# HGRN2 chunk scores: four decay levels in two visits of two levels each, with 88 and 56 query columns

## The chip, the cores and the metric

The kernel runs on one core of a Trainium2 chip. A core has five engines with queues of their own: TensorE (PE, matrix products, with its weight loads shown as PEld), VectorE (DVE), ScalarE (ACT), GpSimd (POOL) and SyncE (SP, which here issues the loads from memory). Their instructions run in the order of each queue and wait for each other through semaphores. Operands lie in the on-chip memory SBUF; TensorE writes its results to PSUM, here in tiles of 128 x 512 that each take a bank, and VectorE and ScalarE read them from there.

The metric is the device time of one launch in microseconds (us); smaller is better.

## The reference: a two-layer trunk, of which the second layer's mixer matters here

The program computes a trunk of two layers on 512 tokens of width 1024: a Mamba-2 mixer, then an HGRN2 mixer, each followed by a normalisation, a squared-ReLU MLP, another normalisation and a gated embedding. Only the HGRN2 mixer is touched. It has 8 heads, 128 wide in keys and in values, and works in chunks of the sequence:

```python
q, fz, v, g = jnp.split(u @ w_in, 4, axis=-1)
log_f = jnp.logaddexp(jnp.log(lb), jnp.log1p(-lb) + jax.nn.log_sigmoid(fz))
k = (1.0 - lb) * jax.nn.sigmoid(-fz)
...
diff = b_[:, :, None] - b_[:, None, :]          # b_: running sum of log_f
dec = jnp.exp(jnp.where(mask, diff, -jnp.inf))
scores = jnp.einsum('blhk,bshk,blshk->bhls', q_, kk, dec)
o = jnp.einsum('bhls,bshv->blhv', scores, v_) + jnp.einsum('blhk,bhkv->blhv', q_ * jnp.exp(b_), s_prev)
```

The score of query token l and key token s (s not after l) is the sum over 128 features of q, k and the product of the forget gates f of the tokens after s up to l. The gates differ by feature, so the decay cannot be taken out of the sum; the outputs are the causal products of scores and values, with a state passed on between chunks.

## The kernel before

Nearly all of the time goes to projections: products of 128 x 128 weights with 512 tokens, each taken as three products of rounded parts (`mm3`, lines 118 to 121, PSUM tiles `pj`). A weight block is loaded (`raw`), rounded by ScalarE (`whi`, line 113), and the remainder is formed by VectorE (`wlo`, line 115).

The HGRN stage runs with an order on TensorE that is written out by hand. `background` (line 903) is one long chain of projections, cut into steps of three matmuls: queries, gates and keys of head h (`qf`), values and output gates (`vg`), and the first half of the output projection (`out0`). `hcore` does the rest for one pair of heads and gives way at each `yield`; the number that it yields (from `FILL`) is how many microseconds' worth of projection steps stand on TensorE before its next part. There are four pairs; for the last one the numbers are multiplied by `LAST`, 0.78. On the other engines a planner sets the order from the program's order, its priorities and the buffers' lives.

`qf` leaves three tiles for a head, all 128 features by 512 tokens: q in a buffer `xs`, the gates f in `sz`, the keys kk in `cv`.

In `hcore` the decay is built up by levels. At level m the tokens stand in blocks of half = 2^m, and neighbouring blocks form a pair. `qd` holds each query times the gates of its own block up to it, kk each key times the gates after it in its block, and `tot` the product of the gates of every block. A key in the first block of a pair and a query in the second one then need no further factor: their scores are a plain matrix product. After level m VectorE multiplies the keys of each first block by the total of the second (line 985), the queries of each second block by the total of the first (line 986), and the totals pairwise (line 988); that makes the state for level m + 1. There are seven levels (half = 1 to 64) in a chunk of 128 tokens.

The products of levels 0 to 4 are done in groups of 32 tokens, 16 groups per head: the keys of a group are the stationary operand (128 x 32), its queries the moving one. I call the 32 matmuls of both heads at one level a visit:

- first visit (line 951): 48 columns, 32 of them the undecayed queries (for the diagonal) and 16 every second one of `qd` (level 0). The two sets lie side by side in the 48-wide `xs` buffer; line 942 copies the 16 into it.
- levels 1 to 4 (line 965): 16 columns each, the second blocks of every pair.
- levels 5 and 6 (line 972): 32 x 32 and 64 x 64 products.

The results go to one PSUM bank per head (`py0`, `py1`). Which of a group's 32 x 32 entries belong to the level is told by a mask: a predicated copy (lines 996 and 1000) takes them from PSUM into `scb`, 128 x 4 x 32 per head. After level 4 ScalarE copies `scb` into the score matrix `sc` (line 1008), and those of levels 5 and 6 come straight from PSUM (line 1014). Then come transposes of the keys (line 1021), the chunk states (lines 1032 to 1037), outputs (lines 1045 to 1047, which read `sc` and `qd`), the norm (lines 1052 to 1057) and transposes of the result (line 1065).

Each level yields 2.94, so that about 12 to 15 projection matmuls stand between two visits, and in that time VectorE does lines 985, 986, 988, 996 and 1000 of the level.

Of the kernel before, what the change touches and what calls it, by code (L numbers as in the profile page):

```python
# [15 lines left out]
P = 128  # L16
# [28 lines left out]
def trunk(ctx: ExitStack, tc, a):  # L45
# [27 lines left out]

    two = dict(xs=2, sz=2, cv=2, cm=2, cbm=2)
    mlp = dict(r=8, blk=2, sg=2)
    bufs = dict(ssd=dict(two, ss=2), mlp0=mlp, hgrn=dict(two, xs=3, sz=4, cv=4, y=2, pv=2, btok=2, sg=2, sc=2, scb=2, qd=2), mlp1=mlp)
    phase = []

    def begin(name):
# [116 lines left out]
        nc.sync.dma_start(b, a["ln"][2 * i + 1 : 2 * i + 2, :].to_broadcast([P, D]))  # L196
        return g, b

    def layer_norm(c, gb, sums=None):

        src = acc[:, c, :]
        mv = mk(sm, [P, 2], "lnmv")
        sd = mk(sm, [P, 1], "lnsd")
        if sums is None:
            st = mk(sm, [P, 2, 6], "lnst")
            for h in range(2):
                nc.vector.bn_stats(st[:, h, :], src[:, h * 512 : (h + 1) * 512])
            nc.vector.bn_aggr(mv, st.rearrange("p a b -> p (a b)"))
            nc.scalar.activation(sd, mv[:, 1:2], AF.Sqrt, bias=eps)
        else:  # L210

            nc.vector.tensor_scalar(mv[:, 0:1], sums[:, c, 0:1], sums[:, c, 1:2], -1.0 / D, ALU.add, ALU.mult)
            sq = mk(sm, [P, 2], "lnsq")
            for h in range(2):
                nc.scalar.activation(
                    tmp("sg", [P, T]), src[:, h * 512 : (h + 1) * 512], AF.Square, bias=mv[:, 0:1], accum_out=sq[:, h : h + 1]
                )
# [60 lines left out]
    def norm(i):  # L278

        gb = ln_params(i)  # L280
        h_s = Split(8)
        sums = mk(sm, [P, NCH, 2], "lnsum") if i else None

        def chunk(c):
            with tc.high_priority(offset=SOON if c < 2 or i % 2 == 0 else 0):
                layer_norm(c, gb, sums)

        return h_s, chunk, lambda c: transpose_split(acc[:, c, :], h_s, c), sums

# [528 lines left out]
    begin("hgrn")  # L818


    lmask = mk(cpool, [P, 6, 32], "lmask", U8)
# [46 lines left out]
    def qf(h):  # L868
        ps = []
        for w in range(2):  # L870
            hi, lo = unit(a["whq"][2 * h + w])
            ps.append(bank(psj, "pj"))
            for k in range(8):
                c = slice(k * P, (k + 1) * P)
                mm3(ps[w], hi[:, c], lo[:, c], x_s.h(k), x_s.l(k), k == 0, k == 7)
                yield 0.65
            if w == 0:

                q = tmp("xs", [P, T // 32, 48])
                nc.scalar.copy(q[:, :, :32], blocks32(ps[0]))  # L880
        f = tmp("sz", [P, T])
        nc.scalar.activation(f, ps[1], AF.Sigmoid)
        nc.scalar.activation(f, f, AF.Identity, scale=lbc[:, h : h + 1], bias=lb[:, h : h + 1])
# [48 lines left out]
    def hcore(h0, s, i0):  # L932
# [3 lines left out]
        q, f, kk = ([need("qf", h0 + r)[n] for r in R] for n in range(3))  # L936
        py = lambda r: bank(psy, "py%d" % r)
        tokens = lambda c, b: (slice(b, b + 32), slice(c * P + b, c * P + b + 32))
        qd = [tmp("qd", [P, T]) for r in R]
        for r in R:  # L940
            nc.vector.tensor_mul(blocks32(qd[r]), q[r][:, :, :32], blocks32(f[r]))
            nc.vector.tensor_copy(q[r][:, :, 32:], blocks32(qd[r])[:, :, 1::2])


        pcs = [py(r) for r in R]
        for r in R:
            for c in range(NCH):
                for b in range(0, P, 32):
                    bs, ts = tokens(c, b)
                    at = slice(c * 48, c * 48 + 48)  # L950
                    nc.tensor.matmul(pcs[r][bs, at], kk[r][:, ts], q[r][:, ts.start // 32], start=True, stop=True)
        tot = f
        tots = [tmp("y", [P, T]) for r in R]
        toff = 0
        for m in range(NLEV):
            half = 1 << m
            if m == NLEV - 2:
                pcs = [py(r) for r in R]
            for r in R if m else ():
                if m < NLEV - 2:  # L960
                    for c in range(NCH):
                        for b in range(0, P, 32):
                            bs, ts = tokens(c, b)
                            at = slice(128 + 64 * m + 16 * c, 128 + 64 * m + 16 * c + 16)
                            nc.tensor.matmul(pcs[r][bs, at], kk[r][:, ts], second(qd[r][:, ts], half), start=True, stop=True)  # L965
                else:

                    for c2 in range(0, NCH, 2):
                        at = slice(base(half) + half * c2 // 2, base(half) + half * (c2 // 2 + 1))
                        for b, c in ((b, c2 + odd) for b in range(0, P, 2 * half) for odd in range(2)):  # L970
                            s0, l0, row = c * P + b, c * P + b + half, b + half * (c - c2)
                            nc.tensor.matmul(
                                pcs[r][row : row + half, at],
                                kk[r][:, s0 : s0 + half],
                                qd[r][:, l0 : l0 + half],
                                start=True,
                                stop=True,
                            )
            nb = T // (2 * half)
            nt = []  # L980
            for r in R:
                qv = qd[r].rearrange("p (b two u) -> p b two u", two=2, u=half)
                kv = kk[r].rearrange("p (b two u) -> p b two u", two=2, u=half)
                tv = tot[r].rearrange("p (b two) -> p b two", two=2)
                nc.vector.tensor_mul(kv[:, :, 0, :], kv[:, :, 0, :], bc(tv[:, :, 1], 2, half))
                nc.vector.tensor_mul(qv[:, :, 1, :], qv[:, :, 1, :], bc(tv[:, :, 0], 2, half))
                nt.append(tots[r][:, toff : toff + nb])
                nc.vector.tensor_mul(nt[r], tv[:, :, 0], tv[:, :, 1])
            toff += nb
            tot = nt  # L990
            for r in R:
                sc, scb, pc = scs[r], scbs[r], pcs[r]
                if m < NLEV - 2:
                    if m == 0:
                        pc = pc[:, : 48 * NCH].rearrange("p (c l) -> p c l", c=NCH)
                        nc.vector.copy_predicated(scb, bc(lmask[:, NLEV - 2, :], 1, NCH), pc[:, :, :32])
                        pc = pc[:, :, 32:]
                    else:
                        pc = pc[:, 128 + 64 * m : 192 + 64 * m].rearrange("p (c l) -> p c l", c=NCH)
                    nc.vector.copy_predicated(  # L1000
                        scb.rearrange("p c (b two u) -> p c b two u", two=2, u=half)[:, :, :, 1, :],
                        bc(second(lmask[:, m, :], half), 1, NCH),
                        pc.rearrange("p c (b u) -> p c b u", u=half),
                    )
                    if m == NLEV - 3:
                        for b in range(0, P, 32):
                            bs = slice(b, b + 32)
                            nc.scalar.copy(sc[bs, :, bs], scb[bs])
                else:
                    pc = pc[:, base(half) : base(half) + 2 * half].rearrange("p (c l) -> p c l", c=2)  # L1010
                    for b in range(0, P, 2 * half):
                        for odd in range(2):
                            row = b + half * odd
                            nc.scalar.copy(sc[b : b + half, odd::2, b + half : b + 2 * half], pc[row : row + half])
            yield FILL[0]

        kt = []
        for r in R:
# [71 lines left out]
def _levels():  # L1090

    i = np.arange(P)
    out = np.zeros((P, 6, 32), np.float32)
    for m in range(5):
        s, l = (i[:, None] % 32) >> m, i[None, :32] >> m
        out[:, m, :] = (s % 2 == 0) & (l == s + 1)
    out[:, 5, :] = i[:, None] % 32 == i[None, :32]
    return out


# [105 lines left out]
```

## Time and profile before

| quantity | value |
|---|---|
| median of 3 runs | 1428.69 us (1428.59 to 1429.52) |
| profiled execution | 1427.82 us, of which the span of the trace is 1426.0 us |
| granted TensorE clock | 1.00 |
| TensorE busy | 1416.5 us, 99% of the span |
| VectorE / ScalarE busy | 1040.9 us / 746.1 us |
| HGRN pairs, about | 833 to 1015 us of the span |

The trace is one execution. A row of the timeline gives start, duration, engine, line, operation, the tiles written and read, shape, and how many equal ones were merged; in brackets stands how long the engine had been idle before it and what ended that. Durations overlap, since an engine begins an instruction before the last one has ended: the distance between two starts tells what an instruction holds its engine for. A single-precision matmul stands in the trace as two records, so a visit of 32 matmuls has 64. A row of the groups gives line, engine, operation, shapes and number, then busy time in all and the mean of one in ns, then the idle time before. A row of waits gives the total, the number and the longest.

### The profile page before, as it was taken

How to read it: one execution, taken by the hardware profiler on the slowest of the kernel's cores; microseconds unless marked ns; L12 is line 12 of the kernel's file. 1: busy time of each engine (PE TensorE's matmuls, PEld its weight loads, DVE VectorE, ACT ScalarE, POOL GpSimd, SP SyncE). 2: the span in 40 equal slices, each digit the busy share in tenths (PEclk: the TensorE clock that was granted, in tenths of full speed). 3: DMA queues.
4: the chain of work that ended last, by engine and by line, in shares of the span. 5: the costliest groups of instructions: out<-in, count | busy, mean ns of one | idle time of the engine just before them, and what ended most of it. 6: DMA issues, size and time to landing. Idle time of an engine off the chain costs nothing.

```text
span 1426.0 us, 20980 instructions
## 1 busy us (share of the span) xinstructions
PE 1416.5 (99%) x8381; PEld 1174.3 (82%) x8381; DVE 1040.9 (73%) x1664; ACT 746.1 (52%) x1118; POOL 1.9 (0%) x12
## 2 busy tenths in 40 slices
PE   9999999999999999999999999999999999999998
PEld 7888888888888888888888878777898888888887
DVE  8998687797967667687977556657685867667873
ACT  7776454563264444545546546555555454544641
POOL 0000000000000000000000000000000000000000
PEclk9999999999999999999999999999999999999999
DMA  8332323233333443434621422122163434434231
GB/s 315 134 124 91 122 84 126 97 118 132 134 119 133 148 141 140 145 136 176 208 74 48 147 76 75 60 90 90 45 234 107 148 133 148 148 133 162 89 119 45
DMA packets 49394, 178.04 MB, mean 125 GB/s; under 512 B 5520, under 2 KB 6288, under 8 KB 49168
## 3 DMA queue, kind: packets, MB, share of 16 engines
q1 hardware_dynamic: 49296, 176.69, 35.3%
q8 instruction: 66, 1.08, 0.3%
q14 instruction: 32, 0.26, 0.1%
HBM read 174.51 MB, written 2.16 MB: 124 GB/s over the span
## 4 chain that ended last, share of the span: by engine, by line
PE 94%; DVE 3%; ACT 2%; DMA 0%; issue 0%; SPq 0%; ACTq 0%; DVEq 0%
PE pj L119 24%; PE pj L120 23%; PE pj L121 23%; PE py L119 5%; PE py L121 5%; PE py L120 5%; PE py L735 1%; PE py L741 1%; PE pm L705 1%; PE py L965 1%; PE pt L233 1%; DVE wlo L115 1%; PE pt L693 1%; PE py L1045 0%; DMA r<-in_w 0%
## 5 line engine op out<-in xcount | busy, mean ns | idle before, releaser
L113 ACT CAST whi<-raw 128x1024 fp32r<-128x1024 f32 x222 | 232.9, 1051 | 346.0 <-PE pj L120 232.8
L119 PE MATMUL pj<-b,whi 128*128 128x512 f32 (+1 forms) x1006 | 382.8, 381 | 0.7 <-ACT b L237 0.7
L120 PE MATMUL pj<-b,whi 128*128 128x512 f32 (+1 forms) x1006 | 380.5, 378 | 0.6 <-DVE b L238 0.6
L121 PE MATMUL pj<-b,wlo 128*128 128x512 f32 (+1 forms) x1006 | 379.3, 377 | 0.0
L115 DVE TENSOR_TENSOR wlo<-raw,whi 128x1024 fp32r<-128x1024 f32 x222 | 269.9, 1220 | 142.2 <-ACT whi L113 136.8
L120 PEld LDWEIGHTS pj<-b,whi 128*128 128x128 f32 x1006 | 189.5, 188 | 33.6 <-issue 0.9
L121 PEld LDWEIGHTS pj<-b,wlo 128*128 128x128 f32 x1006 | 189.4, 188 | 33.7
L119 PEld LDWEIGHTS pj<-b,whi 128*128 128x128 f32 x1006 | 189.0, 188 | 33.9 <-ACT b L237 0.9
L119 PE MATMUL pj<-whi,b 128*128 128x512 f32 x536 | 213.4, 399 | 0.0
L121 PE MATMUL pj<-whi,b 128*128 128x512 f32 x544 | 212.9, 392 | 0.0
L120 PE MATMUL pj<-wlo,b 128*128 128x512 f32 x536 | 210.2, 392 | 0.0
L121 PEld LDWEIGHTS pj<-whi,b 128*128 128x128 f32 x544 | 102.1, 188 | 20.9
L119 PEld LDWEIGHTS pj<-whi,b 128*128 128x128 f32 x536 | 100.8, 188 | 20.6 <-ACT b L1066 0.6
L120 PEld LDWEIGHTS pj<-wlo,b 128*128 128x128 f32 x536 | 100.8, 188 | 19.1
L113 ACT CAST whi<-r 128x1024 fp32r<-128x1024 f32 x72 | 75.7, 1053 | 67.7 <-PE pj L121 38.6
L115 DVE TENSOR_TENSOR wlo<-r,whi 128x1024 fp32r<-128x1024 f32 x72 | 87.7, 1220 | 24.1 <-ACT whi L113 23.6
L121 PE MATMUL py<-whi,b 128*128 128x512 f32 (+1 forms) x250 | 96.9, 388 | 0.0
L120 PE MATMUL py<-wlo,b 128*128 128x512 f32 x224 | 87.2, 389 | 0.0
L119 PE MATMUL py<-whi,b 128*128 128x512 f32 x224 | 87.0, 390 | 0.0
L121 PEld LDWEIGHTS py<-whi,b 128*128 128x128 f32 x250 | 46.9, 188 | 9.7
L634 DVE SCALAR_TENSOR_TENSOR cv<-pj,cst,cv 128x509 f32<-128x509 f32 (+2 forms) x66 | 48.7, 744 | 3.6 <-ACT cv L631 2.8
L119 PEld LDWEIGHTS py<-whi,b 128*128 128x128 f32 x224 | 42.0, 188 | 9.1 <-DVE sg L494 0.3
(284 smaller groups left out, 1828.7 us busy)
## 6 DMA issues: line engine op xcount, KB each, us to landing
raw<-in_w SPq DMA_DIRECT2D x112, 512.0 KB, 3.2
r<-in_w SPq DMA_DIRECT2D x64, 512.0 KB, 3.3
raw<-in_wssd SPq DMA_DIRECT2D x36, 512.0 KB, 3.3
a<-csd SPq DMA_DIRECT2D x16, 512.0 KB, 3.6
raw<-in_wso SPq DMA_DIRECT2D x16, 512.0 KB, 3.2
raw<-in_wg SPq DMA_DIRECT2D x16, 512.0 KB, 3.2
raw<-in_whq SPq DMA_DIRECT2D x16, 512.0 KB, 3.7
raw<-in_whvg SPq DMA_DIRECT2D x14, 512.0 KB, 3.3
```

Of the source, the lines that this page charges most:

```text
L113: nc.scalar.copy(hi[:, :n], f)
L115: nc.vector.tensor_sub(lo[:, :n], f, f32(hi[:, :n]))
L119: nc.tensor.matmul(out, sh, mh, start=start, stop=False, **kw)
L120: nc.tensor.matmul(out, sh, ml, start=False, stop=False, **kw)
L121: nc.tensor.matmul(out, sl, mh, start=False, stop=stop, **kw)
L233: nc.tensor.transpose(pt[:, j * P : (j + 1) * P], src[:, k * P : (k + 1) * P], ident)
L634: nc.vector.scalar_tensor_tensor(cv[:, d:], ps[:, : T - d], convw[:, i, k : k + 1], cv[:, d:], ALU.mult, ALU.add)
L693: nc.tensor.transpose(pt[:, c * P : (c + 1) * P], xs[:, c * P : (c + 1) * P], ident)
L705: nc.tensor.matmul(pst_[:, c * P : (c + 1) * P], btok[:, c, :], xw[:, c].rearrange("p h q -> p (h q)"), start=True, stop=True)
L735: nc.tensor.matmul(yd[64 * r : 64 * r + 64, sl], xdt[:, 2 * c + r, :], m[:, r, sl], start=True, stop=True)
L741: nc.tensor.matmul(yo[:, c * P : (c + 1) * P], pv[:, c - 1].rearrange("p h q -> p (h q)"), cm[:, c * P : (c + 1) * P], start=True, stop=True,)
L965: nc.tensor.matmul(pcs[r][bs, at], kk[r][:, ts], second(qd[r][:, ts], half), start=True, stop=True)
```

## The change

Levels 0 and 1 are taken in one visit, and levels 2 and 3 in another. Seen from blocks of size u (1, then 4), four neighbouring blocks form a group, and a query may lie one, two or three blocks after the key. A query that lies one block later needs what `qd` holds. One that lies two blocks later needs the total of the block between as well, and three blocks later the totals of both. So three sets of queries are laid side by side in a new 88-column tile `near` (tag `qd`): columns 0 to 31 the undecayed queries, 32 to 63 `qd` itself, 64 to 79 the queries of each group's third and fourth block, times one total (`distant`, two products), and 80 to 87 those of the fourth, times two (one more product).

- The first visit has 88 columns (with the undecayed queries), the second 56 (without them); level 4 keeps its 16. There is no visit at levels 1 and 3, and no `yield` after levels 0 and 2; those after 1 and 3 yield twice as much, so the sum is the same.
- In the order of the changed program 27 projection matmuls stand on TensorE between the 88- and the 56-column visit in the first three pairs, and 21 in the last; as many between the 56- and the 16-column one.
- VectorE still multiplies keys, queries and totals at every level, and makes the three products of `distant` twice per head. Its predicated copies are five at level 0, four at level 2 and one at level 4 (six in all before), with eight masks instead of six. The copy of line 942 is gone.
- ScalarE copies q into `near`, and after level 3 the first blocks of `qd` into q's own buffer, where the second blocks are written by the multiplication. From there on q's buffer is `qd`, until the output matmuls. Its buffers become four.
- The second visit takes its own PSUM tile, in the same bank; level 4 writes behind its columns.
- The second norm's squares go to the tag `cbm` instead of `sg`.

```diff
-    bufs = dict(..., hgrn=dict(two, xs=3, sz=4, cv=4, y=2, pv=2, btok=2, sg=2, sc=2, scb=2, qd=2), mlp1=mlp)
+    bufs = dict(..., hgrn=dict(two, xs=4, sz=4, cv=4, y=2, pv=2, btok=2, sc=2, scb=2, qd=2), mlp1=mlp)
...
-                    tmp("sg", [P, T]), src[:, h * 512 : (h + 1) * 512], AF.Square, ...
+                    tmp("cbm" if i == 2 else "sg", [P, T]), src[:, h * 512 : (h + 1) * 512], AF.Square, ...
...
-    lmf = mk(raws, [P, 1024], "raw")[:, :192].rearrange("p (m l) -> p m l", m=6)
+    lmf = mk(raws, [P, 1024], "raw")[:, :256].rearrange("p (m l) -> p m l", m=8)
...
-                q = tmp("xs", [P, T // 32, 48])
-                nc.scalar.copy(q[:, :, :32], blocks32(ps[0]))
+                q = tmp("xs", [P, T])
+                nc.scalar.copy(q, ps[0])
...
-        qd = [tmp("qd", [P, T]) for r in R]
+        near = [tmp("qd", [P, T // 32, 88]) for r in R]
+        qd = [t[:, :, 32:64] for t in near]
         for r in R:
-            nc.vector.tensor_mul(blocks32(qd[r]), q[r][:, :, :32], blocks32(f[r]))
-            nc.vector.tensor_copy(q[r][:, :, 32:], blocks32(qd[r])[:, :, 1::2])
+            nc.vector.tensor_mul(qd[r], blocks32(q[r]), blocks32(f[r]))
+            nc.scalar.copy(near[r][:, :, :32], blocks32(q[r]))
+
+        def distant(r, u):
+            sv = qd[r].rearrange("p k (s f u) -> p k s f u", f=4, u=u)
+            tv = tot[r].rearrange("p (k s f) -> p k s f", k=T // 32, f=4)
+            v2 = near[r][:, :, 64:80].rearrange("p k (s t u) -> p k s t u", t=2, u=u)
+            v3 = near[r][:, :, 80:].rearrange("p k (s u) -> p k s u", u=u)
+            for t in range(2):
+                nc.vector.tensor_mul(v2[:, :, :, t], sv[:, :, :, 2 + t], bc(tv[:, :, :, 1 + t], 3, u))
+            nc.vector.tensor_mul(v3, v2[:, :, :, 1], bc(tv[:, :, :, 1], 3, u))
...
+        wide = {0: 0, 2: 32}
         for m in range(NLEV):
             half = 1 << m
-            if m == NLEV - 2:
+            if m in (0, 2, NLEV - 2):
                 pcs = [py(r) for r in R]
-            for r in R if m else ():
-                if m < NLEV - 2:
+            for r in R if m in wide else ():
+                distant(r, half)
+            for r in R:
+                if m in wide:
+                    n = 88 - wide[m]
                     for c in range(NCH):
                         for b in range(0, P, 32):
                             bs, ts = tokens(c, b)
-                            at = slice(128 + 64 * m + 16 * c, 128 + 64 * m + 16 * c + 16)
-                            nc.tensor.matmul(pcs[r][bs, at], kk[r][:, ts], second(qd[r][:, ts], half), start=True, stop=True)
+                            qs = near[r][:, ts.start // 32, wide[m] :]
+                            nc.tensor.matmul(pcs[r][bs, n * c : n * c + n], kk[r][:, ts], qs, start=True, stop=True)
+                elif m < NLEV - 3:
+                    pass
+                elif m == NLEV - 3:
...
+                            at = slice(224 + 16 * c, 240 + 16 * c)
+                            nc.tensor.matmul(pcs[r][bs, at], kk[r][:, ts], qd[r][:, ts.start + 16 : ts.stop], start=True, stop=True)
...
+                    if m == 3:
+                        nc.scalar.copy(new[:, :, :, 0], old[:, :, :, 0])
+                        qd[r] = q[r]
...
+                    if m in wide:
...
+                        if m == 0:
+                            keep(scb, lmask[:, 0], pc[:, :, :32])
+                        pc = pc[:, :, 32 - wide[m] :]
+                        m0 = 1 + 3 * (m // 2)
+                        keep(scb, lmask[:, m0], pc[:, :, :32])
...
+                        for t in range(2):
+                            keep(sv[:, :, :, 2 + t], mv[:, m0 + 1, :, 2 + t], v2[:, :, :, t])
+                        keep(sv[:, :, :, 3], mv[:, m0 + 2, :, 3], pc[:, :, 48:].rearrange("p c (s u) -> p c s u", u=u))
+                    elif m == NLEV - 3:
+                        pc = pc[:, 224:288].rearrange("p (c l) -> p c l", c=NCH)
+                        keep(scb[:, :, 16:], lmask[:, 7, 16:], pc)
...
-            yield FILL[0]
+            if m != 0 and m != 2:
+                yield FILL[0] * (2 if m in (1, 3) else 1)
```

More of the change, by code (lines that the diff above doesn't have):

```diff
@@ L197, in ln_params, with layer_norm @@
         return g, b
-    def layer_norm(c, gb, sums=None):
+    def layer_norm(i, c, gb, sums=None):
         src = acc[:, c, :]
@@ L1092, in _levels @@
     i = np.arange(P)
[L1093 to L1097, printed above, removed]
+    out = np.zeros((P, 8, 32), np.float32)
+    s, l = i[:, None] % 32, i[None, :32]
+    out[:, 0, :] = s == l
+    for n, u in ((1, 1), (4, 4)):
+        for d in range(3):
+            out[:, n + d, :] = (s // u == l // u - d - 1) & (s // (4 * u) == l // (4 * u))
+    out[:, 7, :] = (s < 16) & (l >= 16)
     return out
```

46 lines of the change are left out of this document (22 added, 24 removed).

## The prediction

> **What bounds the kernel now.** I read the page's totals first, then its chain that ended last.
>
> ```profile
> span 1426.0 us, 20980 instructions
> PE 1416.5 (99%) x8381; PEld 1174.3 (82%) x8381; DVE 1040.9 (73%) x1664; ACT 746.1 (52%) x1118; POOL 1.9 (0%) x12
> PE 94%; DVE 3%; ACT 2%; DMA 0%; issue 0%; SPq 0%; ACTq 0%; DVEq 0%
> ```
>
> TensorE sets the time: whatever leaves its queue shortens the kernel, and every wait put into it lengthens it. Next, the HGRN stage by stretches (first and fourth pair of heads), and what PE waited for from 815 to 1020 us.
>
> ```profile
> 833.40:881.00 47.60, 46.89 (x575) 38.14 (x575) 28.92 (x81) 26.01 (x65) 0.00 (x0) 1.00 0.21 72
> 965.00:1015.00 50.00, 49.16 (x599) 39.20 (x597) 34.85 (x91) 26.98 (x79) 0.00 (x0) 1.00 0.26 86
> PE py L972 <- ACT sc L1014: 0.7, 2, 0.4
> PE pt L1065 <- DVE b L1067: 0.6, 1, 0.6
> PE pt L1021 <- ACT btok L1023: 0.6, 1, 0.6
> PE py L965 <- DVE scb L1000: 0.2, 1, 0.2
> ```
>
> Columns of the first two: length, then busy time of PE, PEld, DVE, ACT. The clock is 1.00 in both. PE lost about 2 us to waits in all four pairs; VectorE is busy 28.9 of 47.6 us and 34.9 of 50.0, so it has room on average, least in the fourth pair.
>
> **What a visit costs today.** A visit is the 32 small score matmuls of both heads (64 records), set between projection matmuls. Timeline of PE, first pair:
>
> ```profile
> 829.03 0.39 PE L121 MATMUL pj<-b,wlo 128*128 128x512 f32 x1
> ...
> 833.11 0.39 PE L121 MATMUL pj<-b,wlo 128*128 128x512 f32 x1
> 833.43 0.89 PE L951 MATMUL py<-xs,cv 128*32 128x48 f32 x64
> 834.25 0.50 PE L119 MATMUL pj<-b,whi 128*128 128x512 f32 x1
> 834.58 0.40 PE L120 MATMUL pj<-b,whi 128*128 128x512 f32 x1
> ...
> 836.87 0.39 PE L121 MATMUL pj<-b,wlo 128*128 128x512 f32 x1
> 837.19 0.74 PE L965 MATMUL py<-qd,cv 128*32 128x16 f32 x64
> ...
> 841.50 0.74 PE L965 MATMUL py<-qd,cv 128*32 128x16 f32 x64
> ...
> 845.13 0.74 PE L965 MATMUL py<-qd,cv 128*32 128x16 f32 x64
> ...
> 849.44 0.74 PE L965 MATMUL py<-qd,cv 128*32 128x16 f32 x64
> ...
> 853.05 0.46 PE L972 MATMUL py<-qd,cv 128*32 128x32 f32 x32
> ...
> L951 PE MATMUL py<-xs,cv 128*32 128x48 f32 x256 | 3.6, 208 | 0.0
> L965 PE MATMUL py<-qd,cv 128*32 128x16 f32 x1024 | 11.8, 185 | 0.2 <-DVE scb L1000 0.2
> L972 PE MATMUL py<-qd,cv 128*32 128x32 f32 x128 | 1.8, 199 | 0.0
> ```
>
> Undisturbed, 18 projection matmuls take 833.11 - 829.03 = 4.08 us, 0.2267 each. From visit to visit stand 12, 15, 12, 15 and 12 of them. What is left over is the price of the visit: 837.19 - 833.43 - 12 x 0.2267 = 1.04 us for the 48-column one, and 0.91, 0.91, 0.91, 0.89 for the four of 16: 4.66 us per pair. A price splits into records and a rest: (0.89 - 0.208) / 63 = 10.9 ns a record at 48 columns, (0.74 - 0.185) / 63 = 8.8 ns at 16; 64 records are 0.70 and 0.56 us, and both times 0.345 us stays for going to small tiles and back.
>
> **The visits after the change.** Levels 0 and 1 share an 88-column visit, 2 and 3 a 56-column one, level 4 keeps its 16: three visits for five; the two above (L972) stay. The wide prices are in no row. The lower bound continues the line from 16 to 48 columns (0.13 us per 32): 1.20 and 1.07 us. The upper bound takes the record as proportional to its columns from 48 on: 19.9 and 12.7 ns, so 0.345 + 64 x 0.0199 = 1.62 and 1.16 us. I take the upper one: 8.8 ns at 16 columns and 8.4 at 32 ((0.46 - 0.199) / 31, L972) is a floor, and 48 already stands above it. New sum 1.62 + 1.16 + 0.90 = 3.68 us; per pair 0.98 us is saved, 3.9 us over four pairs.
>
> The Trainium skill, "TensorEngine Tiling (Array Packing)", section Instruction Overhead, says that a matmul has some 60 cycles of overhead, so that one column takes as long as 60. By that rule the 56-column visit would cost what one of 16 does and the 88-column one 88/60 of its records, and some 6.7 us would go instead of 3.9 (nearest to the third rival below). The trace bears it out only in part: 16 and 32 columns cost alike, 48 do not.
>
> **VectorE between the first two visits.** Here the saving can be lost: the 56-column visit waits for work that was spread over two gaps and has grown. Rows of VectorE today (one of ScalarE's at the end):
>
> ```profile
> 828.59 0.69 DVE L941 TENSOR_TENSOR qd<-xs,sz 128x512 f32<-128x512 f32 x1 [0.45 <-ACT sz L883]
> ...
> 834.04 0.43 DVE L985 TENSOR_TENSOR cv<-cv,sz 128x256 f32<-128x256 f32 x1 [0.46 <-PE py L951]
> 834.39 0.30 DVE L996 COPY_PREDICATED scb<-lmask,py 128x128 f32<-128x128 uint8 x1
> 834.59 0.42 DVE L985 TENSOR_TENSOR cv<-cv,sz 128x256 f32<-128x256 f32 x1
> 834.92 0.29 DVE L1000 COPY_PREDICATED scb<-lmask,py 128x64 f32<-128x64 uint8 x1
> 835.05 0.30 DVE L996 COPY_PREDICATED scb<-lmask,py 128x128 f32<-128x128 uint8 x1
> ...
> 842.02 0.42 DVE L985 TENSOR_TENSOR cv<-cv,y 128x256 f32<-128x256 f32 x1 [1.09 <-PE py L965]
> 842.36 0.42 DVE L986 TENSOR_TENSOR qd<-qd,y 128x256 f32<-128x256 f32 x1
> 842.70 0.42 DVE L985 TENSOR_TENSOR cv<-cv,y 128x256 f32<-128x256 f32 x1
> ...
> 981.30 0.69 DVE L901 SCALAR_TENSOR_TENSOR acc<-acc,pj 128x512 f32<-128x512 f32 x1 [1.53 <-PE pj L121]
> 981.91 0.42 DVE L985 TENSOR_TENSOR cv<-cv,y 128x256 f32<-128x256 f32 x1
> ...
> 988.28 1.23 DVE L115 TENSOR_TENSOR wlo<-raw,whi 128x1024 fp32r<-128x1024 f32 x1 [1.32 <-ACT whi L113]
> 989.42 0.42 DVE L985 TENSOR_TENSOR cv<-cv,y 128x256 f32<-128x256 f32 x1
> ...
> L1000 DVE COPY_PREDICATED scb<-lmask,py 128x64 f32<-128x64 uint8 x40 | 8.1, 252 | 0.1
> L942 DVE COPY xs<-qd 128x256 f32<-128x256 f32 x8 | 2.3, 282 | 0.1
> L988 DVE TENSOR_TENSOR y<-y 128x128 f32<-128x128 f32 x8 | 2.3, 287 | 0.1
> ...
> 845.96 0.58 ACT L880 COPY xs<-pj 128x512 f32<-128x512 f32 x1
> ```
>
> Independent operations start before the last has ended: a multiplication of 256 elements holds the queue 0.335 us (842.02 to 842.70, two of them; 0.42 long), a copy of 128 0.20, of 64 0.13, L901 0.61, L115 1.14. Time from the start of the 88-column visit: its first head is done after 32 x 0.0199 = 0.64, and VectorE begins 0.26 later (834.04 - 833.43 less 32 x 0.0109), at 0.90. Then, in the changed program's order: eight multiplications (levels 0 and 1, keys and queries, two heads) 2.68; four predicated copies of 128 0.80 and six of 32 elements at no more than the 0.13 of 64, 0.78; and the six products for the decayed queries two and three blocks away, 128 elements each, 1.20 by the 0.20 of the 128-element copy. The first head's last product is the fourth: issued at 5.76, done by its 0.29 us at 6.05. The last is done at 6.45, or 7.6 in the first two pairs, where an L115 stands before it.
>
> PE in the same gap: streaming 1.27, 0.13 to the next projection (834.25 - 833.43 - 0.70), 27 projections in the first three pairs (0.33, then 0.23 each), 0.32 to the visit: first half at 7.80, second 0.41 later at 8.2. Slack is 1.75 us for the first head, 0.6 at least for the second. In the fourth pair 21 projections bring the visit to 6.42, and an L901 stands before the products: 6.66 for the first head, so PE waits 0.3 us with the semaphore's way; the second head (7.06) is then in time. In the second gap the chain is 0.67 + 2.68 + 0.40 + 0.78, and two ScalarE copies of at most 0.6 each, some 5.8 us against 7.3 due (6.0 in the fourth pair): nothing.
>
> **The rest, beside PE.** Per head VectorE loses one L942 (0.28) and gains six products and four small copies (1.2 + 0.5): 11 us over the stage, into its idle 15 to 19 us per pair. ScalarE gains two copies per head, of 512 and 256 elements, together under two L880 (1.2 us), 9 us in all, into 21 of 47.6 us idle. The products ahead of the first visit are done in the pair before, and in the first pair between L941 at 828.6 and the visit at 833.4: L941 and two more multiplications' worth, under 2 us. The query buffers (four for three) are now held until the output matmuls, so head 4's copy out of PSUM waits for them; its bank is wanted again only after the three other banks have filled, 48 matmuls on: nothing. The bank of the second visit is free once the first visit's copies are done, at about 5.2 of 7.8. The mask's load is 32 KB longer, its conversion 64 columns (0.07 us), both at a time when PE has weights ahead; the norm's change of buffer moves no instruction. If VectorE's cover were gone, each microsecond of lateness would cost PE one, up to four times.
>
> **Sum:** -3.9 + 0.3 = -3.6 us. The profiled execution took 1427.82 us (span 1426.0), 0.87 under the median 1428.69; it would go to 1424.2 and the median to 1425.1.
>
> **Rivals.**
> 1. VectorE somewhat later than its rows say: the new shapes have steps of four and eight columns. With the chain 1 us longer PE waits 0.4 us in each of the first two pairs, none in the third, 1.3 in the fourth: 2.1 in all, 1426.9. For it: slack of 0.6 and less than none. Against it: L985 takes 0.42 to 0.43 both where its step is two elements (834.04) and where it is eight (842.02).
> 2. Slower: the operations follow each other by their whole durations, since many depend on the one before. First gap 0.90 + 8 x 0.42 + 4 x 0.30 + 6 x 0.25 + 6 x 0.29 = 8.7 us; PE waits 1.7 in each of the first two pairs (with L115), 0.5 in the third, 2.6 in the fourth (with L901); in the second gap 1.3 more there. 7.8 - 3.9: 1432.6. It decides from a sum of 3.9 us on, about 1 us per pair. Against it: the early starts in the rows above, though the operations there do not depend on each other. The Trainium skill, "VectorE: DVE Perf Modes", section The DRAIN you can't avoid, has the next operation start only when the pipeline is empty, and points to another section for those that start earlier; the rows above show the earlier start.
> 3. Wide columns are cheap: the lower bound, 4.66 - 1.20 - 1.07 - 0.90 = 1.49 per pair, 6.0 in all; the visit then comes sooner and PE waits some 0.6 in the fourth pair: 1423.3. Against it: 48 columns are above the floor.
>
> **How the numbers follow.** Forecast 0.57 (own range 1424.1 to 1426.3), rival 1 0.22, rival 2 0.13, rival 3 0.08. 0.2% is 2.9 us, about what a measurement of this kernel tells from no change: faster is under 1425.8. That is most of the forecast and rival 3: 0.55; same, the rest of the forecast and rival 1: 0.32; slower, rival 2: 0.13. The range runs from rival 3 past rival 1: 1423.0 to 1430.0, rival 2 and a little of the rest left out.
>
> **What would show it.** The 88-column visit with 64 records in about 1.5 us and 56-column ones in 1.0; two fewer visits per pair; no wait of PE on VectorE's query tile before the 56-column visit in pairs one to three and under 0.5 us in the fourth. Wrong if that wait is a microsecond per pair, if the wide records take more than 20 ns, or if the first projection after a visit comes later than 0.13 us behind its records.

## The result, and the profile after

The changed kernel took 1425.9 us (median of 11 runs, 1424.0 to 1426.31) where the kernel before took 1428.69 (11 runs, 1427.99 to 1430.28): the ratio is 0.9976, with an interval of 0.9967 to 0.9985, so 0.24% faster. (The ratio goes by all the runs; the two medians by themselves are 0.20% apart.) The profiled execution took 1424.0 us, the shortest of the 11; its span is 1422.2 us, 3.8 under that of before.

The page of the changed kernel: span, busy time by engine, and the shares of the chain that ended last.

```profile
span 1422.2 us, 20042 instructions
PE 1412.7 (99%) x7869; PEld 1172.5 (82%) x7869; DVE 1055.1 (74%) x1736; ACT 754.2 (53%) x1134; POOL 1.9 (0%) x12
PE 94%; DVE 2%; ACT 2%; DMA 1%; issue 0%; ACTq 0%; DVEq 0%
```

TensorE still sets the time. It has 512 records fewer (8381 to 7869) and is busy 3.8 us less: two visits of 64 records, four times. VectorE and ScalarE got more to do, and neither has become the bound.

What PE waited for from 815 to 1020 us, by line and releaser:

```profile
PE py L987 <- ACT sc L1046: 0.7, 2, 0.4
PE pt L1098 <- DVE b L1100: 0.6, 1, 0.6
PE pt L1054 <- ACT btok L1056: 0.6, 1, 0.6
PE py L972 <- DVE qd L953: 0.4, 1, 0.4
```

The first three stood there before, under other line numbers. The wait of 0.2 us on `scb` is gone, and one of 0.4 us on the products of `distant` (line 953) is new.

PE's timeline, the first pair of heads (start, duration):

```profile
833.59 1.42 PE L972 MATMUL py<-qd,cv 128*32 128x88 f32 x64
834.94 0.50 PE L119 MATMUL pj<-b,whi 128*128 128x512 f32 x1
...
841.28 0.99 PE L972 MATMUL py<-qd,cv 128*32 128x56 f32 x64
...
848.54 0.73 PE L980 MATMUL py<-xs,cv 128*32 128x16 f32 x64
...
852.17 0.46 PE L987 MATMUL py<-xs,cv 128*32 128x32 f32 x32
```

Between the visits stand 27, 27 and 12 projections of 0.2267 us. The prices follow as in the prediction: 841.28 - 833.59 - 6.12 = 1.57 us for 88 columns, 848.54 - 841.28 - 6.12 = 1.14 for 56, 852.17 - 848.54 - 2.72 = 0.91 for 16. Their sum is 3.62 us against 4.66, so a pair saves 1.04 us.

To compare kernels without what happens elsewhere in the program I use one **stage measure**: from the first visit of pair 1 to the first 32 x 32 visit (level 5) of pair 4. Before it runs from 833.43 to 994.65, 161.22 us; after from 833.59 to 991.07, 157.48 us. The stage gained 3.74 us, practically the whole difference of the spans.

### The profile page after: what moved, and what is told of

The parts are those of the page before. It is cut to its first block, busy times and chain, and to the rows that moved or that the text cites. A ratio compares the mean times of both kernels' runs of the same rounds, so it can differ in the third digit from the quotient of the medians.

```text
span 1422.2 us, 20042 instructions
## 1 busy us (share of the span) xinstructions
PE 1412.7 (99%) x7869; PEld 1172.5 (82%) x7869; DVE 1055.1 (74%) x1736; ACT 754.2 (53%) x1134; POOL 1.9 (0%) x12
## 4 chain that ended last, share of the span: by engine, by line
PE 94%; DVE 2%; ACT 2%; DMA 1%; issue 0%; ACTq 0%; DVEq 0%
PE pj L119 24%; PE pj L120 24%; PE pj L121 24%; PE py L119 5%; PE py L121 5%; PE py L120 5%; PE py L735 1%; PE pt L233 1%; PE py L741 1%; PE pm L705 1%; DMA raw<-in_wssd 1%; PE py L972 1%; PE pt L693 1%; PE py L1078 1%; DVE wlo L115 0%
## 5 line engine op out<-in xcount | busy, mean ns | idle before, releaser
L115 DVE TENSOR_TENSOR wlo<-raw,whi 128x1024 fp32r<-128x1024 f32 x222 | 270.0, 1221 | 126.4 <-ACT whi L113 124.6
L115 DVE TENSOR_TENSOR wlo<-r,whi 128x1024 fp32r<-128x1024 f32 x72 | 87.7, 1220 | 20.6 <-ACT whi L113 19.9
```

The costliest lines, as they stand in the source:

```text
L115: nc.vector.tensor_sub(lo[:, :n], f, f32(hi[:, :n]))
```

## The experiments

The theory was the prediction's: a visit costs 0.345 us plus 64 records, which take time in proportion to their columns above a floor, and VectorE's products are hidden except in pair 4. The rivals were its three: a later VectorE chain, operations that follow each other by whole durations, and cheap wide columns. All start from the changed kernel, and each is compared with the kernel before on the same chip.

**The changed kernel once more (again)**, no edit.

> The changed kernel once more, for a second execution of it in a trace and a closer ratio. If the saving is what the first pair of traces shows (3.8 us between spans of 1426.0 and 1422.2), the ratio comes out near 0.9973 and the span near 1422 to 1423. If that trace caught a short execution and the medians (1428.69 and 1425.9, 2.8 us) are nearer the truth, the ratio is near 0.9980 and the excess stands in no visit. Either way the visits cost 1.57, 1.14 and 0.91 us per pair and PE waits 0.4 us in the fourth pair for the products of the decayed queries.

Measured: 1425.89 us against 1429.04, ratio 0.9978 (0.997 to 0.9987). The profiled execution has a span of 1425.1 us, 2.9 more than the first one, yet its stage is 157.49 us, from 835.99 to 993.48. Of the 2.9 us, 2.4 lie ahead of the stage, nearly all in the first 46 us of the span, where among other things PE waited longer:

```profile
PE pt L693 <- ACT btok L662: 0.9, 1, 0.9
PE pt L660 <- DVE toks L625: 0.5, 1, 0.5
```

In the first profiled execution the first of these is 0.2 and the second is not in the list, so these two explain 1.2 of the 2.4 us. Single executions of the same program thus differ by up to 3 us outside of what was changed. The stage repeats within 0.01 us in these two executions of the changed kernel (of the kernel before there is one trace), and I read the experiments by it.

**Only the first merge (only01)**: levels 0 and 1 in one visit of 88 columns; levels 2, 3 and 4 keep their visits of 16.

```diff
-        wide = {0: 0, 2: 32}
+        wide = {0: 0}
...
-                elif m < NLEV - 3:
+                elif m < 2:
                     pass
+                elif m in (2, 3):
+                    ... # 16 columns per group, as before
```

> Only levels 0 and 1 share a visit (88 columns); levels 2, 3 and 4 have 16 columns each. Theory (a visit costs 0.345 us and 64 records, each at least 8.8 ns and else in proportion to its columns): 1.57 + 3 x 0.91 = 4.30 us per pair for 4.66 before, 1.4 us less in all and some 0.2 for the wait on the predicated copies that goes, near 1427 by the median. Rival (a dropped visit is worth the same whatever the others' columns, half of the 1.04 us that a pair saved): 0.52 per pair, 2.1 in all. No wait of PE on VectorE between the first two visits, since the six products of levels 2 and 3 are gone.

Measured: 1428.23 us, ratio 0.9993 (0.9985 to 1.0002). The stage is 159.43 us, 1.79 under before, and PE never waits for the products. By the prices: 1.04 + 0.91 - 1.57 = 0.38 per pair, 1.52 over four, and 0.24 from the wait on `scb` that this version does not have either: 1.76. The rival's 2.1 us, to which the same 0.24 would come, are not there.

**Only the second merge (only23)**: level 0 in a visit of 64 columns (the undecayed queries and all of `qd`), level 1 in 16, levels 2 and 3 in 56.

```diff
-        wide = {0: 0, 2: 32}
+        wide = {2: 32}
...
+                elif m < 2:
+                    ... # level 0: near[:, :, :64]; level 1: 16 columns
```

> Only levels 2 and 3 share a visit (56 columns); level 0 has 64 columns (the undecayed and the decayed queries side by side), levels 1 and 4 have 16. Theory: 0.345 + 64 x 0.0141 = 1.25, and 0.91, 1.14, 0.91: 4.21 per pair, 1.8 us less than before in all, if nothing waits. But now only 12 to 15 projections (2.7 to 3.4 us) lie ahead of the 56-column visit, and the products for it come behind level 1's multiplications: some 3.4 us of VectorE, 4.6 where a weight remainder stands among them, against 3.7 to 4.4: PE waits up to 0.5 us in some pairs, and the saving falls to 0.5 to 1.8 us. Rival (VectorE is hidden anyhow): the full 1.8 and no wait before the 56-column visit.

Measured: 1428.02 us, ratio 0.9996 (0.9987 to 1.0005); stage 160.42 us, 0.80 under before. PE's waits in this kernel:

```profile
PE py L972 <- DVE qd L953: 0.9, 2, 0.6
```

The 64-column visit costs 837.49 - 833.52 - 12 x 0.2267 = 1.25 us. The prices alone would save 4 x (4.66 - 1.25 - 0.91 - 1.14 - 0.90) = 1.84 us, and the `scb` wait that is gone here too 0.24; the products, which now have one gap instead of two, take 1.28 of that back, all of it in pairs 3 and 4 (0.76 and 0.50 us), where the waits shown stand. The two merges by themselves give 1.79 + 0.80 = 2.59 us, both at once 3.74. What lies between: this version pays 4 x (1.25 - 1.04) = 0.84 us for its first visit, and its late products cost 0.6 us more than the full change's 0.68 (products0, below), while the `scb` wait counts twice in the 2.59. So the double gap behind the first merge decides in pair 3, where only 12 projections stand ahead of the 56-column visit of this version: there it hides products that cost 0.76 us here. In pairs 1 and 2 the 15 projections of the single gap hide them as well, and in pair 4 they are late in both versions.

**The cost of columns by itself (wide112)**: the second visit streams its 56 columns twice over, 112 in all, the second half into columns that nobody reads.

```diff
-                    n = 88 - wide[m]
+                    n = 88 if m == 0 else 112
...
+                            if m == 2:
+                                qs = bc(qs, 1, 2)
```

> The changed kernel with the 56 columns of the second visit streamed twice (112 columns; the second 56 results are not read). Theory (records in proportion to their columns, some 0.2 ns per column and record by the visits of 56 and 88): the visit goes from 1.14 to 1.86 us, 0.72 more per pair, 2.9 us in all. Rival (the price of a visit lies in the number of its matmuls, columns cost little): under 0.3 us per pair, about 1 in all.

Measured: 1428.62 us, ratio 0.9996 (0.9987 to 1.0006): the gain is gone. PE's timeline, the first pair:

```profile
842.32 1.74 PE L974 MATMUL py<-qd,cv 128*32 128x112 f32 x64
...
850.33 0.73 PE L982 MATMUL py<-xs,cv 128*32 128x16 f32 x64
```

The visit's price is 850.33 - 842.32 - 6.12 = 1.89 us. The stage is 2.72 us longer than that of the changed kernel, where 4 x (1.89 - 1.14) would be 3.0: in pair 4 the visit and the gap behind it are only 0.52 longer instead of 0.75, since the longer first half hides the late products of the second head. With this all prices stand side by side:

| columns | 16 | 48 | 56 | 64 | 88 | 112 |
|---|---|---|---|---|---|---|
| price of a visit, us | 0.91 | 1.04 | 1.14 | 1.25 | 1.57 | 1.89 |

From 48 columns up they lie on one line, (1.89 - 1.04) / 64 = 0.0133 us a column. Followed downwards the line meets 0.91 at 48 - (1.04 - 0.91) / 0.0133 = 38 columns. By this estimate a column costs nothing up to there and its full price above; the records of 16 and 32 columns in the prediction (8.8 and 8.4 ns) lie on the floor, and between 32 and 48 nothing was measured. That settles rival 3. What the floor and the 0.345 us are made of, no run here shows. The Trainium skill, "TensorEngine Tiling (Array Packing)", section Instruction Overhead, gives each matmul an overhead of about 60 cycles. If it made a visit of 56 columns cost as much as one of 16, the table would have 0.91 where it has 1.14; by the measurements the floor exists, but it ends near 38 columns here.

**The products earlier on VectorE (prio)**: a higher priority for `distant` of the second visit.

```diff
-                distant(r, half)
+                with tc.high_priority(offset=SOON if m else 0):
+                    distant(r, half)
```

> The changed kernel with the products for levels 2 and 3 at a higher priority on VectorE: in each pair the first head's three come ahead of the second head's last multiplication, and in the fourth pair ahead of the output projection's addition. If the 0.4 us wait of the fourth pair comes from that addition, it falls to 0.2 us or less; nothing else moves, and the time stays within 0.1% of the changed kernel. If the wait has another cause, it stays at 0.4.

Measured: 1425.01 us (9 runs), ratio 0.9977 (0.9967 to 0.9986). The stage is 157.25 us, 0.23 less than that of the changed kernel, and the wait in pair 4 is 0.3 instead of 0.4 us. Neither of the two expected values came out, because the wait has moved: the planner now puts L901 behind the first head's products, but still ahead of the second's last one. The first head's wait is gone (from the 88- to the 56-column visit it is 6.34 us, where the changed kernel has 6.82), and the addition, 0.61 us of the chain, was enough to cause it; the 0.3 us are the second head's. In total time the two versions can't be told apart. Its profiled execution is the longest of its nine (1428.54 us) although its stage is shorter than the changed kernel's; the section on the hardware says what its trace shows.

**The products two and three times over (products2, products3)**, which make VectorE's chain ahead of the second visit longer:

```diff
-                distant(r, half)
+                for _ in range(2 if m == 2 else 1):   # products3: 3
+                    distant(r, half)
```

> The changed kernel with the six products for the second visit formed twice (the same values again), 1.2 to 1.8 us more for VectorE in the gap between the first two visits. Theory (slack of the second head 0.5 us in the first two pairs, some 1.6 in the third, none in the fourth): PE waits 0.7 to 1.3 us longer in each of the first two pairs, 0 to 0.2 in the third and 1.2 to 1.8 in the fourth: 2.6 to 4.6 us more in all. Rival (VectorE has room, as it is idle a third of the stage): no change.

> The same products formed three times, 2.4 to 3.6 us more for VectorE in that gap. Theory: 1.9 to 3.1 us of waiting in each of the first two pairs, 0.8 to 2 in the third, 2.4 to 3.6 in the fourth beyond today's 0.4: 7 to 12 us in all, from here on about a microsecond of PE per microsecond of VectorE in every pair. Rival (room): under 2 us.

Measured: 1430.45 us, ratio 1.0007 (0.9997 to 1.0016), with the products taken twice, and 1443.55, ratio 1.01 (1.0085 to 1.0115), with them three times. PE's wait for them, in products2 and then in products3:

```profile
PE py L973 <- DVE qd L953: 4.2, 5, 1.2
```

```profile
PE py L973 <- DVE qd L953: 10.3, 6, 2.1
```

PE's timeline of products2, the second visit of pair 1:

```profile
842.62 0.60 PE L973 MATMUL py<-qd,cv 128*32 128x56 f32 x32
843.92 0.60 PE L973 MATMUL py<-qd,cv 128*32 128x56 f32 x32 [0.69 <-DVE qd L953]
```

In products2 the first two pairs wait 0.69 and 0.68 us, and each is 0.87 us longer than in the changed kernel (47.92 and 47.72 us from first visit to first visit, against 47.05 and 46.85). The wait is the smaller number because it falls into the middle of a visit: it is counted from the end of the first half's records, 0.60 us behind their start, while the second half would have followed after 0.4. Six more products of 0.20 us make the chain 1.2 us longer, so the changed kernel had about 0.33 us of slack there. The prediction's 0.6 left out the semaphore's way, which takes 0.15 us (843.49 + 0.28 = 843.77 is the end of the last product in pair 1, 843.92 the start of PE's second half).

In the third pair I had expected at most 0.2 and got 1.23. VectorE's timeline there (the 88-column visit starts at 930.57):

```profile
930.83 1.23 DVE L115 TENSOR_TENSOR wlo<-raw,whi 128x1024 fp32r<-128x1024 f32 x1 [0.76 <-ACT whi L113]
931.97 0.42 DVE L1000 TENSOR_TENSOR cv<-cv,sz 128x256 f32<-128x256 f32 x1
...
938.12 0.50 DVE L952 TENSOR_TENSOR qd<-qd,y 128x128 f32<-128x128 f32 x2
938.52 1.23 DVE L115 TENSOR_TENSOR wlo<-raw,whi 128x1024 fp32r<-128x1024 f32 x1
939.66 0.29 DVE L953 TENSOR_TENSOR qd<-qd,y 128x128 f32<-128x128 f32 x1
```

Two weight remainders (L115) touch the chain. The first holds its start back to 1.40 us behind the visit, where 0.88 is usual, a loss of 0.52; it does so in the changed kernel too (a start at 928.91 behind a visit at 927.49), where slack hides it. The second stood behind the last product in the changed kernel; here the longer chain runs into it, so that it stands ahead of the last product, as it does in pairs 1 and 2. So the wait should be that of pair 1 and the later start, 0.69 + 0.52 = 1.21 us; I had left out both remainders in this pair.

The stage of products2 is 4.36 us longer than that of the changed kernel, that of products3 15.7; the waits have grown by 3.8 and 9.9. For products2 4.36 lies within the 2.6 to 4.6 expected, but partly by luck: pair 3 is 1.46 us longer where I had at most 0.2, and pair 4, at 1.16, lies a little under its range. For products3 the waits lie within the 7 to 12 us expected and the stage does not. What products3 lost beside its waits is in the section on the hardware.

**No products at all (products0)**: `distant` is not called for the second visit, so this kernel leaves out the scores of levels 2 and 3 for queries two and three blocks away.

```diff
-            for r in R if m in wide else ():
+            for r in R if m == 0 else ():
                 distant(r, half)
```

> The changed kernel without the six products for the second visit: the scores of levels 2 and 3 for queries two and three blocks away then use what levels 0 and 1 left in the tile, so that part of the computation is left out. Theory: only the wait of 0.4 us in the fourth pair goes, and perhaps 0.3 us with it; the other pairs have slack already. Rival (the products hold PE up in every pair in some way that no wait shows): about 1 us per pair.

Measured: 1425.43 us, ratio 0.9971 (0.9961 to 0.9982). The stage is 156.77 us, 0.71 under that of the changed kernel, more than the wait of 0.41. PE's timeline of pair 4, first in products0, then in the changed kernel:

```profile
975.90 1.42 PE L972 MATMUL py<-qd,cv 128*32 128x88 f32 x64
...
982.24 0.99 PE L972 MATMUL py<-qd,cv 128*32 128x56 f32 x64
...
988.15 0.74 PE L980 MATMUL py<-xs,cv 128*32 128x16 f32 x64
```

```profile
974.51 1.42 PE L972 MATMUL py<-qd,cv 128*32 128x88 f32 x64
...
981.33 1.20 PE L972 MATMUL py<-qd,cv 128*32 128x56 f32 x64 [0.41 <-DVE qd L953]
...
987.44 0.74 PE L980 MATMUL py<-xs,cv 128*32 128x16 f32 x64
```

From the 88- to the 56-column visit it is 6.34 us without and 6.82 with the products: the first head's lateness costs 0.48. From there to the next visit it is 5.91 and 6.11: 0.20 more, and the visit's own records take 1.20 instead of 0.99 us, so the second head is late as well (its matmuls start at 981.86, 0.53 behind the first half instead of 0.4). That is 0.68 in pair 4, and all of the stage's 0.71 but 0.03: in pairs 1 to 3 the products cost nothing.

## Why the prediction was right, step by step

The time came out at 1425.9 us where 1425.1 was forecast, and faster by 0.24%; the likeliest case is the one that happened, and the range held it. By the medians alone it stands right at the border: 1425.9 where the prediction called "faster" what is under 1425.8.

- **The visits.** The upper of the two bounds was the right one: 1.57 us at 88 columns (1.62 forecast), 1.14 at 56 (1.16), 0.91 at 16 (0.90). A record took (1.42 - 0.24) / 63 = 18.7 ns and (0.99 - 0.215) / 63 = 12.3 ns, against 19.9 and 12.7. The saving was 1.04 us per pair, 4.16 in all, not 3.9. Proportion through the origin, fixed at 48 columns, was slightly too steep.
- **The way back to projections.** The first one starts 834.94 - 833.59 - 64 x 0.0187 = 0.15 us behind the records; 0.13 was forecast, and anything later was named as a sign of being wrong. Taken literally that sign is there, by 0.02 us. Nothing hangs on it: the price of the visit holds this way, and it came out lower than forecast.
- **VectorE's chain in the first gap.** Its row by row sum came out almost to the hundredth. VectorE's timeline of the changed kernel, pair 1:

```profile
834.47 0.43 DVE L999 TENSOR_TENSOR cv<-cv,sz 128x256 f32<-128x256 f32 x1 [0.73 <-PE py L972]
834.81 0.42 DVE L1004 TENSOR_TENSOR qd<-qd,sz 128x256 f32<-128x256 f32 x1
...
838.76 0.69 DVE L952 TENSOR_TENSOR qd<-qd,y 128x128 f32<-128x128 f32 x3
839.37 0.29 DVE L953 TENSOR_TENSOR qd<-qd,y 128x128 f32<-128x128 f32 x1
839.57 0.29 DVE L952 TENSOR_TENSOR qd<-qd,y 128x128 f32<-128x128 f32 x1
839.77 1.22 DVE L115 TENSOR_TENSOR wlo<-raw,whi 128x1024 fp32r<-128x1024 f32 x1
840.91 0.29 DVE L953 TENSOR_TENSOR qd<-qd,y 128x128 f32<-128x128 f32 x1
```

  Counted from the visit at 833.59, it begins at 0.88 (0.90 forecast), the first head is done at 839.37 + 0.29 = 839.66, 6.07 (6.05), and the second at 841.20, 7.6 (7.6). The visit comes at 7.69 instead of 7.80 and its second half 0.4 later. Of this 0.11 us the cheaper visit makes 0.05; the rest is a rounding in the prediction, which added up projections of 0.23 instead of 0.2267 us. The slack of the second head is 0.5 us (0.6), or 0.33 once the semaphore's way of 0.15 us is taken off.
- **The fourth pair.** The right wait in the right place for the right reason, but mis-sized: 0.3 us forecast, 0.68 measured. The rows of VectorE there:

```profile
979.68 0.69 DVE L901 SCALAR_TENSOR_TENSOR acc<-acc,pj 128x512 f32<-128x512 f32 x1
980.28 0.70 DVE L952 TENSOR_TENSOR qd<-qd,y 128x128 f32<-128x128 f32 x3
980.89 0.29 DVE L953 TENSOR_TENSOR qd<-qd,y 128x128 f32<-128x128 f32 x1
981.09 0.29 DVE L952 TENSOR_TENSOR qd<-qd,y 128x128 f32<-128x128 f32 x1
981.42 0.29 DVE L953 TENSOR_TENSOR qd<-qd,y 128x128 f32<-128x128 f32 x1
```

  The first head is done 981.18 - 974.51 = 6.67 us after the visit, as forecast (6.66), and PE goes on 0.15 us later, where the forecast had some 0.06 for that way. And the visit was due at 6.34, not 6.42 (the cheaper visit and the rounding above). Together that is 0.48 us instead of 0.3. The second head, which I had in time at 7.06, is done at 981.71, 7.20, and PE's second half needs it 0.4 behind the first, at 7.22: with the same 0.15 us of way it is late too, and costs the other 0.20. Nearly all of the 0.14 us between 7.06 and 7.20 stands in the last two rows. The last product reads the result of the one right before it and starts 0.33 us behind that one, where I had counted 0.20 for every product.
- **The sum of the stage.** -4.16 + 0.68 - 0.24 (the wait on `scb` that went, which I had not credited) = -3.72; the stage measure says -3.74. The forecast's -3.6 holds three small errors, -0.26, +0.38 and -0.24, that nearly cancel: that the sum fits so closely is partly luck.
- **From the stage to the median.** I moved the median by what the profiled execution would lose. The two medians of the comparison differ by 2.8 us, those of the second one (again) by 3.15, and the second interval, 1.9 to 4.3 us, holds 3.74. The part that scatters lies outside the stage, in the two traces of the changed kernel mostly ahead of it.
- **The work beside PE.** In the same stretch VectorE is busy 16.9 us more, where I had 11, and ScalarE 7.0 more, where I had 9 (833 to 1020 us, before and after: length, then busy time of PE, PEld, DVE, ACT):

```profile
833.00:1020.00 187.00, 184.86 (x2281) 148.28 (x2280) 116.00 (x315) 100.20 (x251) 0.00 (x0) 1.00 0.22 75
```

```profile
833.00:1020.00 187.00, 184.66 (x1784) 149.38 (x1783) 132.94 (x391) 107.20 (x267) 0.00 (x0) 1.00 0.22 74
```

  Some of it is the 3.7 us of later work that the stretch now takes in: over the stage alone (833.43 to 994.65 before, 833.59 to 991.07 after) VectorE is busy 13.7 us more and ScalarE 6.5. Beyond the wait of pair 4 it cost nothing: no other wait of PE names it. Nor did the second gap, the query buffers or the PSUM bank bring one.

**The rivals.** The later chain (1) was wrong about the steps of four and eight columns: the products of the first head hold VectorE 0.20 us each as the 128-element copy did. The slower case (2) fell, for nearly all of the chain, in the same rows: multiplications of 0.42 us started 0.34 us apart (834.47 to 834.81), products of 0.29 us 0.20 apart (839.37 to 839.57). The order takes the two heads in turn, so that an operation's operands mostly come from two operations before. Where one reads the result of the operation right before it, the rival's mechanism does show: the second head's last product starts 0.33 us behind the one whose result it reads in pair 4 (981.09 to 981.42), and 0.31 in pair 3 of the changed kernel:

```profile
934.07 0.28 DVE L952 TENSOR_TENSOR qd<-qd,y 128x128 f32<-128x128 f32 x1
934.38 0.29 DVE L953 TENSOR_TENSOR qd<-qd,y 128x128 f32<-128x128 f32 x1
```

In the traces of again, only23, wide112 and products2 such neighbours are 0.31 or 0.32 us apart. So here an operation of 0.28 or 0.29 us was over before the one that reads its result began. The rival had that for the whole chain, 2.25 us more; in pair 4 it holds for one product, 0.13 us more. The Trainium skill, "VectorE: DVE Perf Modes", section The DRAIN you can't avoid, lets the next operation start only when the pipeline is empty and points to another section for those that start earlier; most rows here are of the earlier kind, and these pairs begin behind the end. How near this rival was can be read from products2: with the chain 1.2 us longer the gain was gone (a ratio of 1.0007). The cheap columns (3) fell with wide112.

## What to carry to other kernels

Before merging small matmuls, measure what a visit costs at two widths, above and below the floor: a merge saves the whole price of a narrow visit (0.91 us here) and pays for every column that it adds above the floor's end (about 38 here, 0.0133 us each). What is merged needs its operands earlier, so add up the other engine's chain row by row, by distances between starts, with the whole duration where an operation reads the result of the one right before it, and with every foreign instruction that the planner puts into it (here one weight remainder of 1.14 us decides between slack and wait). And judge such a change by the span of its own stage: that repeated within 0.01 us in two executions, whose whole spans differ by 2.9.

## What the runs showed of the hardware

**A wait can cost more than itself.** In products3 the waits grew by 9.9 us and the stage by 15.7. Most of the rest is the clock that TensorE was granted. Stretches of 3.41 us in products3 (length, busy time of PE, PEld, DVE, ACT, POOL, then the granted clock):

```profile
840.73:844.14 3.41, 1.93 (x38) 1.23 (x36) 3.41 (x14) 1.76 (x3) 0.00 (x0) 1.00 0.01 2
...
891.93:895.34 3.41, 1.33 (x56) 1.07 (x45) 3.41 (x11) 0.41 (x1) 0.00 (x0) 1.00 0.28 73
895.34:898.75 3.41, 3.41 (x9) 2.65 (x8) 3.41 (x14) 2.39 (x4) 0.00 (x0) 0.50 0.23 88
898.75:902.17 3.42, 3.42 (x16) 2.79 (x15) 3.00 (x8) 0.00 (x0) 0.00 (x0) 1.00 0.49 153
...
943.13:946.54 3.41, 1.33 (x65) 1.13 (x65) 3.41 (x11) 0.41 (x1) 0.00 (x0) 1.00 0.13 30
946.54:949.95 3.41, 3.41 (x9) 2.67 (x9) 3.38 (x15) 1.65 (x3) 0.00 (x0) 0.50 0.33 126
...
990.91:994.33 3.42, 1.78 (x8) 1.13 (x6) 3.42 (x15) 0.00 (x0) 0.00 (x0) 1.00 0.00 0
994.33:997.74 3.41, 1.67 (x66) 1.45 (x67) 3.34 (x16) 0.41 (x1) 0.00 (x0) 1.00 0.00 0
997.74:1001.15 3.41, 3.41 (x9) 2.63 (x8) 2.55 (x11) 0.53 (x2) 0.00 (x0) 0.50 0.03 5
```

Three times the granted clock is 0.50 for exactly such a stretch and 1.00 on both sides of it. The second and third of them start (946.54 and 997.74) 15 and 30 stretches behind the first (895.34), so in this trace the stretches stand on a fixed grid. The halved ones follow a stretch in which PE was busy less than half (1.33, 1.33 and 1.67 of 3.41 us); after 1.78 and 1.93 the clock stayed. The same wait of 2.08 us halved nothing in pair 1, where a border of the grid at 844.14 divides it. At half the clock a stretch should do half its work, an estimated loss of 1.7 us. The visits agree: from the second half of the 56-column visit to the next visit PE took 6.88 us in pair 1 and 8.51 in pair 2, 1.63 more. So 3 x 1.7 + 9.9 = 15.0 of the 15.7 us are told; the rest is about what a wait in the middle of a visit costs beyond its own length (0.87 for 0.69 us in products2), four times. The same is in the profiled execution of prio, far behind the stage, after a single wait of 1.7 us:

```profile
1045.87:1049.28 3.41, 1.67 (x14) 1.47 (x13) 2.96 (x3) 0.00 (x0) 0.00 (x0) 1.00 1.03 419
1049.28:1052.69 3.41, 3.41 (x18) 3.41 (x18) 3.00 (x3) 1.54 (x2) 0.00 (x0) 0.50 0.36 141
```

The wait and the 1.7 us behind it make 3.4 us; the execution lies 3.5 above the median of its nine. The other eight left no trace, so that this is the reason is likely and not shown. The Trainium skill, "TensorE: Matmul & The Clock Gate", section What's actually happening, has a free-running window of 3413 ns and a clock of one half or the whole; both agree with these rows. Its advice, in the section Why this matters for your kernels, to avoid idle gaps of PE above some 3 us is too lenient here: 1.7 us in one window was enough. The border at half of a window is read from six windows; no run was made for it alone.
